# Top-k searches by bisection: the sample's with one bit a round on ScalarE alone, the prompt's as separate chains on VectorE and on ScalarE with GpSimd

## The chip, the cores and the metric

One core of one Trainium2 chip runs the kernel. The metric is device microseconds of one launch, from start to end; the median of three runs is given. One execution more was run with the hardware profiler; its durations, waits and starts are what the prediction works with. A core has five engines that each work through a list of instructions in order: TensorE (PE, matrix products), VectorE (DVE), ScalarE (ACT, functions of one input), GpSimd (POOL) and SyncE (SP, transfers). GpSimd also issues the indirect gathers. An instruction waits at the head of its engine's list until what it needs is there, and all that stands behind it waits with it.

## The reference

One inference step of a layer with two groups of heads on the same normalised input of 1024 prompt tokens and 32 sample tokens (8 sequences of 4). Group A is attention over the 256 keys with the highest index score; group B is retention, chunk by chunk. Cut to what matters here:

```python
def _index_select(qi, wi, ki, qpos, kpos, topk):
    s = jnp.einsum('bqhd,bsd->bqhs', qi, ki) * (D_IDX ** -0.5)
    score = jnp.einsum('bqh,bqhs->bqs', wi, jax.nn.relu(s))
    valid = kpos[None, None, :] <= qpos[None, :, None]
    score = jnp.where(valid, score, -jnp.inf)
    top_val, top_idx = lax.top_k(score, topk)
    return top_idx, jnp.isfinite(top_val)
```

For the prompt, a query block of 128 tokens has 128 to 1024 keys; for the sample, each of 32 queries has 8192 cached keys, read by page, and its new ones. The chosen keys go into a softmax attention; of retention only the chunked products matter here: each of four head pairs projects queries and keys, then values and gates, for 8 token blocks and the sample.

## The kernel before, in words

The whole is one function, `tile_step`. A scheduler that simulates the kernel while it is built lists the instructions of each engine; what is written under `tc.high_priority()` is preferred. The stages by time: normalisation, transposes, the index projections and the prompt's index scores (`index_scores`, to about 176 us); the **key stage** (176 to 348), which gathers the sample's cached index keys; **retention** (348 to 641), four head pairs; the sample's selection and both attentions (from 593 to 840, overlapping retention's end); the output projection and the gates at the end.

**The prompt's search.** `bisect_prompt` (L618) is a generator, `bp`, that finds for each of 128 rows in 6 query blocks (384, 512, 640, 768, 896 and 1024 keys wide, `NB`) the 256th largest score, bit by bit. The scores' upper halves are copied as bf16 to `x16` and searched in 15 rounds; the lower halves of the scores that equal the result so far, as `y16`, in 16 rounds. In a round, `count` (L631) counts for each block the scores that reach the block's test value: the two largest blocks (`NA`) on ScalarE, as a Sign whose sum is accumulated (L644), the other four on VectorE (L648). VectorE turns the sums of signs into counts (L652, with the constant `halfn`) and then moves the test values of all six blocks in one go (L667 and L669; L690 to L693). So both engines meet in each round. Behind the search stands a mask for each block.

**The key stage.** A loop over 8 batches and two halves (L768) gathers 128x2048 of keys on GpSimd into `kx` (L772, two buffers), transposes them on TensorE (L782), copies them on ScalarE to `kT` (L783), multiplies them by the index queries (`pox`, L786) and applies relu on ScalarE (L789). `head_sum` and `by_key` sum over heads and write the scores to memory. Between, `unit` runs the projections `pb` (L252 to L254) of attention, and each half steps `bp` by about 1.5 rounds.

**The sample's search.** `bisect_sample` (L807), the generator `bss`, loads the scores as 128 partitions of 2080 (each query's on four partitions and for 8 batches) and does the same search twice over 16 bits. A round finds two bits with three test values: two Signs on ScalarE over all 2080 (L844), with their bias made by an Identity each (L865) from values that GpSimd prepares (L870 and L877), and for the middle value three counts on VectorE over 704, 688 and 688 (`jv`, L883) with one small step each (L887). A matmul with a constant 128x128 matrix (`totals`, `stot`, L849) adds up the partitions of a query, a Sign on the totals (L893) tells which tests hold, and VectorE moves the middle (L894). Eight rounds make a search.

**Retention.** For each head pair (L1368) the projection passes `pqk` (L262 to L264, three products each, 8 token blocks) with rotary steps on VectorE (L973 to L975) and GpSimd (L977, L978), then `pvg` with gates on ScalarE (L988) and the chunk products (L994 to L1005, L1395 to L1406). After each token block, `steps(hp)` (L1354) steps a search: in head pair 0 one of `bss` and two of `bp`, later one of `ss`. What is left of `bp` and of `bss` is written out when head pair 1 begins.

**The selection.** `sample_select` (L1097), the generator `ss`, starts from the found threshold: comparisons of all scores (L1133, L1134), prefix sums by a scan (L1142) and matmuls (`pfx`, L1148), corrections (L1156 to L1165), products `pdf` (L1175), then a loop of 11 rounds that makes the list of chosen keys (`oh` L1185, `psl` L1187, `le` L1191, L1195 to L1199). The list drives the gathers of cached keys and values (L1086) for the sample's attention, which runs mixed with the prompt's (L1471 to L1531).

Of the kernel before, what the change touches and what calls it, by code (L numbers as in the profile page):

```python
# [10 lines left out]
F32 = mybir.dt.float32  # L11
# [9 lines left out]
T = 1024  # L21
# [21 lines left out]
def _const_table():  # L43
# [36 lines left out]
    put("halfn", np.tile((np.arange(3, 9) * 64.0)[None, :], (128, 1)))  # L80
# [40 lines left out]
def tile_step(ctx: ExitStack, tc: tile.TileContext, I, O):  # L121
# [496 lines left out]
    def bisect_prompt():  # L618
# [16 lines left out]
        V = nc.vector  # L635

        def count(src, thr, op, scale=None):


            for j, o, n in lens[::-1]:  # L640
                t = thr if isinstance(thr, float) else thr[:, j:j + 1]
                if scale and j >= NB - NA:
                    js = bs.tile([128, 2 * T], BF16, tag="rk", bufs=1, name="js")
                    nc.scalar.activation(js[:, :n], src[:, o:o + n], AF.Sign, bias=t, scale=-scale,  # L644
                                         accum_out=cnt[:, j:j + 1])
                    continue
# [3 lines left out]
            if scale:  # L650
                a = slice(NB - NA, NB)
                V.scalar_tensor_tensor(cnt[:, a], cnt[:, a], -0.5, C("halfn")[:, a], op0=ALU.mult, op1=ALU.add)  # L652

# [9 lines left out]
        V.tensor_scalar(cand, tb_, 1 << 30, None, op0=ALU.bitwise_xor)  # L663
        for bit in range(30, 15, -1):
            count(x16, cand.bitcast(F32), ALU.is_ge, 1.0 + 2.0 ** -10)

            V.tensor_scalar(gb, cnt, float(TOPK), float(1 << bit), op0=ALU.is_lt, op1=ALU.mult)  # L667
            if bit > 16:
                V.scalar_tensor_tensor(cand, gb, 1 << (bit - 1), cand, op0=ALU.bitwise_xor, op1=ALU.bitwise_xor)  # L669
            else:  # L670
                V.tensor_tensor(tb_, cand, gb, op=ALU.bitwise_xor)
            yield
# [14 lines left out]
        V.memset(cf, float(1 << 15))  # L687
        for bit in range(15, -1, -1):
            count(y16, cf, ALU.is_ge, 1.0 + 2.0 ** -18)
            V.tensor_tensor(ge, cnt, need, op=ALU.is_ge)  # L690
            V.scalar_tensor_tensor(v, ge, float(1 << bit), v, op0=ALU.mult, op1=ALU.add)
            if bit:
                V.tensor_scalar(cf, v, float(1 << (bit - 1)), None, op0=ALU.add)  # L693
            yield
# [112 lines left out]
    def bisect_sample():  # L807
# [15 lines left out]
        nc.sync.dma_start(jk.bitcast(F32)[:, :128], I["const"][:, CW + 384:CW + 512])  # L823
        groupr = ss_.tile([128, 128], F32R, name="groupr")
        nc.gpsimd.tensor_copy(groupr, jk.bitcast(F32)[:, :128])
        group = groupr.bitcast(F32)
        cand, gb = (bits[:, i:i + 1] for i in range(2))
        sm = ss_.tile([128, 11], F32, name="ssm")
        cnt, sg, ng, c65, tu, v, need, te, k1, k2, bias = (sm[:, i:i + 1] for i in range(11))
        sgn = ss_.tile([128, 4], F32R, name="sgn")  # L830
# [3 lines left out]
        def count(thr, op):  # L834
# [3 lines left out]
            nc.tensor.matmul(t, group, cnt, start=True, stop=True)  # L838
            return t

        def signs(src, bias, j):

            with nc.allow_low_precision(reason="whole numbers up to NX"):
                nc.scalar.activation(jk, src, AF.Sign, bias=bias, accum_out=sgn[:, j:j + 1])  # L844

        def totals():

            t = bank("stot", "t")[:, 0:4]
            nc.tensor.matmul(t, groupr, sgn, start=True, stop=True)  # L849
            return t  # L850

        def search(src, k, mid):


            s = float(1 << 14)
            b = None
            V.memset(mid, 2 * s - 0.5)
            pre = ss_.tile([128, 4], F32, tag="pre", bufs=2, name="pre")
            for j in range(2):
                nc.gpsimd.memset(pre[:, j:j + 1], 0.5 - (3 - 2 * j) * s)  # L860
            for r in range(8):
                if r:
                    b = pre[:, 2:4]
                    for j in range(2):
                        nc.scalar.activation(b[:, j:j + 1], up, AF.Identity, bias=pre[:, j:j + 1], scale=-2.0 * s)  # L865
                        signs(src, b[:, j:j + 1], j)
                    if r < 7:
                        pre = ss_.tile([128, 4], F32, tag="pre", bufs=2, name="pre")
                        for j in range(2):
                            nc.gpsimd.tensor_scalar(pre[:, j:j + 1], b[:, j:j + 1], 0.75 * s * (1 - 2 * j), None,  # L870
                                                    op0=ALU.add)
                else:
                    for j in range(2):
                        signs(src, pre[:, j:j + 1], j)
                    p0, pre = pre, ss_.tile([128, 4], F32, tag="pre", bufs=2, name="pre")
                    for j in range(2):
                        nc.gpsimd.tensor_scalar(pre[:, j:j + 1], p0[:, j:j + 1], 0.75 * s * (1 - 2 * j), None,  # L877
                                                op0=ALU.add)
                c2 = ss_.tile([128, 5], F32, tag="c2", bufs=2, name="c2")
                part = -float(NX)  # L880
                for j, c, w in ((0, 0, 704), (1, 704, 688), (2, 1392, 688)):
                    jv = ss_.tile([128, 704], BF16, tag="jv", bufs=1, name="jv")
                    V.tensor_scalar(jv[:, :w], src[:, c:c + w], mid, None, op0=ALU.is_ge, op1=ALU.add,  # L883
                                    accum_out=c2[:, j:j + 1])
                    to = c2[:, 3 + j:4 + j] if j < 2 else sgn[:, 2:3]
                    with nc.allow_low_precision(reason="whole numbers up to NX"):
                        V.tensor_scalar(to, c2[:, j:j + 1], 2.0, part, op0=ALU.mult, op1=ALU.add)  # L887
                    part = to
                t = totals()

                st = ss_.tile([128, 4], F32, tag="st4", bufs=2, name="st4")
                up = st[:, 3:4]
                nc.scalar.activation(st[:, 0:3], t[:, 0:3], AF.Sign, bias=k, accum_out=up)  # L893
                V.scalar_tensor_tensor(mid, up, s / 2, mid, op0=ALU.mult, op1=ALU.add)  # L894
                s /= 4
                yield
# [8 lines left out]
        yield from search(u16, k1, tu)  # L905
        V.tensor_scalar(bias, tu, -1.0, -0.5, op0=ALU.mult, op1=ALU.add)
        signs(u16, bias, 0)
        t = totals()[:, 0:1]
# [10 lines left out]
        yield from search(u16, k2, v)  # L919
# [10 lines left out]
        nc.tensor.matmul(tot, group, cnt, start=True, stop=True)  # L930
# [8 lines left out]
        sel, eq, rk = (jk.bitcast(F32)[:NS, i * NS:i * NS + NS] for i in range(3))  # L939
# [414 lines left out]
    def steps(hp):  # L1354

        with tc.high_priority():
            step(bss if hp == 0 else ss)
# [385 lines left out]
```

## Time and profile before

| | before |
|---|---|
| three runs | 1080.88, 1080.19, 1079.3 us (median 1080.19) |
| profiled execution: its time, and its span | 1084.95 us, 1083.1 us |
| granted TensorE clock, mean | 0.964 |
| TensorE busy | 1005.3 us (93%) |
| weight loads | 845.4 us (78%) |
| VectorE busy | 765.1 us (71%) |
| ScalarE busy | 572.4 us (53%) |
| GpSimd busy | 292.4 us (27%) |
| instructions | 20067 |

A row that names a group (`L844 ACT ACTIVATE sjk<-su,pre`) has the line, the engine, the operation, and the tile written from the tiles read. In rows of one tile, `203/208/1322` are the shortest, the median and the longest in ns, then the first and the last start. In a row of waits, the engine and line that waited stands before `<-`, what ended the wait behind it. In tables by stretch, the columns follow the engines in the order of the table above, each with busy us and the number of instructions; then the granted clock, the share of the DMA engines and GB/s. The share of an engine over the whole span is a mean over stages that have different limits.

### The profile page before, as it was taken

How to read it: one execution, taken by the hardware profiler on the slowest of the kernel's cores; microseconds unless marked ns; L12 is line 12 of the kernel's file. 1: busy time of each engine (PE TensorE's matmuls, PEld its weight loads, DVE VectorE, ACT ScalarE, POOL GpSimd, SP SyncE). 2: the span in 40 equal slices, each digit the busy share in tenths (PEclk: the TensorE clock that was granted, in tenths of full speed). 3: DMA queues.
4: the chain of work that ended last, by engine and by line, in shares of the span. 5: the costliest groups of instructions: out<-in, count | busy, mean ns of one | idle time of the engine just before them, and what ended most of it. 6: DMA issues, size and time to landing. Idle time of an engine off the chain costs nothing.

```text
span 1083.1 us, 20067 instructions
## 1 busy us (share of the span) xinstructions
PE 1005.3 (93%) x7377; PEld 845.4 (78%) x7377; DVE 765.1 (71%) x2262; ACT 572.4 (53%) x1216; POOL 292.4 (27%) x301
## 2 busy tenths in 40 slices
PE   3899997988998889999999986899999799999998
PEld 2899997766776788888888954566665799999998
DVE  6847778989889998968769879677663622683332
ACT  5545564976798356877832335555554432442210
POOL 3102223111201532424425215544331421122110
PEclk9999999989999999999999975899999899999999
DMA  8211235536343311300321544434211511332211
GB/s 285 65 59 50 78 107 176 180 116 203 125 161 103 74 40 40 80 18 26 79 81 25 141 119 110 133 87 115 58 50 61 144 60 40 115 125 81 84 41 41
DMA packets 98308, 102.24 MB, mean 94 GB/s; under 512 B 21346, under 2 KB 88386, under 8 KB 95906
## 3 DMA queue, kind: packets, MB, share of 16 engines
q1 hardware_dynamic: 92450, 74.74, 23.2%
q0 software_dynamic: 5760, 26.22, 7.8%
q8 instruction: 58, 0.95, 0.4%
q14 instruction: 40, 0.33, 0.1%
HBM read 79.25 MB, written 21.68 MB: 93 GB/s over the span
## 4 chain that ended last, share of the span: by engine, by line
PE 67%; DVE 14%; issue 6%; ACT 6%; DMA 4%; POOL 2%; SPq 0%; POOLq 0%; DVEq 0%; ACTq 0%
PE pb L252 4%; PE pb L253 4%; PE pb L254 4%; PE pg L262 3%; PE pg L264 3%; PE pg L263 3%; PE ob L1519 3%; PE ptp L1511 2%; PE pvg L262 2%; PE po L262 2%; PE po L263 2%; PE pvg L264 2%; PE po L264 2%; PE pox L786 2%; PE pvg L263 2%
## 5 line engine op out<-in xcount | busy, mean ns | idle before, releaser
L1086 POOL DMA_INDIRECT kvs<-in_cache_kv,idx x64 | 63.2, 987 | 87.1 <-ACT pT L1516 39.2
L262 PE MATMUL pqk<-whi_qkb,xh 128*128 128x256 f32 x256 | 74.3, 290 | 3.5 <-DVE rp L975 3.2
L262 PE MATMUL po<-whi_o,yTh 128*128 128x256 f32 x256 | 74.0, 290 | 3.9 <-DVE x L1606 3.4
L262 PE MATMUL pvg<-whi_vgb,xh 128*128 128x256 f32 x256 | 75.2, 294 | 1.1 <-ACT sg L988 1.1
L264 PE MATMUL pvg<-whi_vgb,xl 128*128 128x256 f32 x256 | 74.7, 292 | 0.0
L264 PE MATMUL pqk<-whi_qkb,xl 128*128 128x256 f32 x256 | 73.9, 289 | 0.0
L263 PE MATMUL pvg<-wlo_vgb,xh 128*128 128x256 f32 x256 | 73.7, 288 | 0.0
L264 PE MATMUL po<-whi_o,yTl 128*128 128x256 f32 x256 | 73.7, 289 | 0.0
L263 PE MATMUL pqk<-wlo_qkb,xh 128*128 128x256 f32 x256 | 73.5, 287 | 0.0
L263 PE MATMUL po<-wlo_o,yTh 128*128 128x256 f32 x256 | 73.3, 287 | 0.0
L262 PE MATMUL pg<-whi_g,yTh 128*128 128x256 f32 x256 | 72.7, 284 | 0.0
L264 PE MATMUL pg<-whi_g,yTl 128*128 128x256 f32 x256 | 72.3, 282 | 0.0
L263 PE MATMUL pg<-wlo_g,yTh 128*128 128x256 f32 x256 | 72.2, 282 | 0.0
L844 ACT ACTIVATE sjk<-su,pre 128x2080 bf16<-128x2080 uint16 x32 | 64.8, 2025 | 5.0 <-DVE su L903 4.7
L1504 ACT ACTIVATE L<-L,mn 128x128 f32<-128x128 f32 (+7 forms) x64 | 49.5, 775 | 20.9 <-DVE mn L1501 17.7
L1700 DVE TENSOR_TENSOR sgm<-pu,sgm 128x256 f32<-128x256 f32 x32 | 13.6, 424 | 64.5 <-PE pu L264 55.3
L497 DVE SCALAR_TENSOR_TENSOR score<-r,wi,score 128x384 f32<-128x384 f32 (+5 forms) x42 | 44.2, 1052 | 20.7 <-ACT r L493 19.6
L262 PEld LDWEIGHTS pqk<-whi_qkb,xh 128*128 128x128 f32 x256 | 49.0, 191 | 7.4 <-issue 4.9
L262 PEld LDWEIGHTS po<-whi_o,yTh 128*128 128x128 f32 x256 | 49.9, 195 | 5.6 <-DVE x L1606 3.6
L1516 ACT COPY pT<-ptp 128x512 f32<-128x512 f32 x54 | 31.3, 581 | 41.9 <-PE ptp L1511 33.4
L648 DVE TENSOR_SCALAR_CACHE_REDUCE jk<-mask,cf 128x768 bf16<-128x768 uint16 (+1 forms) x64 | 51.9, 812 | 2.0
L1699 ACT ACTIVATE sgm<-pg 128x256 f32<-128x256 f32 x32 | 12.3, 383 | 75.9 <-PE pg L264 67.8
(525 smaller groups left out, 3471.3 us busy)
## 6 DMA issues: line engine op xcount, KB each, us to landing
wraw_qkb<-in_w_in SPq DMA_DIRECT2D x16, 256.0 KB
wraw_vgb<-in_w_in SPq DMA_DIRECT2D x16, 256.0 KB
wraw_o<-in_w_out SPq DMA_DIRECT2D x8, 512.0 KB
qas<-qas_d SPq DMA_DIRECT2D x8, 512.0 KB
xr<-in_x_prompt SPq DMA_DIRECT2D x8, 512.0 KB
wraw_g<-in_w_ple_gate SPq DMA_DIRECT2D x8, 512.0 KB
out_y_prompt<-sgm SPq DMA_DIRECT2D x32, 128.0 KB
qas_d<-qst SPq DMA_DIRECT2D x8, 384.0 KB
```

Of the source, the lines that this page charges most:

```text
L252: nc.tensor.matmul(pt[:m, :n], wh, xh[:, k, ts], start=(k == 0), stop=False)
L253: nc.tensor.matmul(pt[:m, :n], wh, xl[:, k, ts], start=False, stop=False)
L254: nc.tensor.matmul(pt[:m, :n], wl, xh[:, k, ts], start=False, stop=(k == KC - 1))
L262: nc.tensor.matmul(pt[:, :n], ah, hi[:, k, :n], start=(k == 0), stop=False)
L263: nc.tensor.matmul(pt[:, :n], ah, lo[:, k, :n], start=False, stop=False)
L264: nc.tensor.matmul(pt[:, :n], al, hi[:, k, :n], start=False, stop=(k == kc - 1))
L497: nc.vector.scalar_tensor_tensor(sc, r[:, :n], wi[:, qb, h:h + 1], sc, op0=ALU.mult, op1=ALU.add)
L648: V.tensor_scalar(jk[:, :n], src[:, o:o + n], t, None, op0=op, op1=ALU.add, accum_out=cnt[:, j:j + 1])
L844: nc.scalar.activation(jk, src, AF.Sign, bias=bias, accum_out=sgn[:, j:j + 1])
L1086: return nc.gpsimd.indirect_dma_start(out=dst, out_offset=None, in_=kvflat, in_offset=bass.IndirectOffsetOnAxis(ap=idx, axis=0))
L1504: behind[0] = nc.scalar.activation(L[:, :n], L[:, :n], AF.Exp, bias=least, scale=-1.0, accum_out=sm[:, i4:i4 + 1])
L1519: nc.tensor.matmul(ob[64 * o:64 * o + 64, :256], vtok[:, kb, kv * 64:kv * 64 + 64], pT[:, o * 256:o * 256 + 256], start=(kb == 0), stop=(k ...
```

## The change

**The prompt.** `count` serves the four small blocks on VectorE alone, and VectorE moves only their test values. Each of the two large blocks has a chain of its own: ScalarE's Sign accumulates into a column of a new tile `lt`, and GpSimd makes the next test value in three small steps (128x1): it adds the next bit, makes from the sum of signs what has to be taken back, and takes it back. The test value lies in two columns by turns (`tst`, in the second search `low2`). The bits' values are in `dl`, made from the constant `pow2`, which takes `halfn`'s place.

**The sample.** A search has 16 rounds of one bit. A round is one Sign over 2080 on ScalarE, the matmul `stot`, a Sign on its column and an Identity that makes the next bias, both on ScalarE too. The counts and the middle on VectorE and the steps on GpSimd go. The step of `bss` in `steps` is two rounds in head pair 0.

**Small things.** `group` has a tile and a load of its own with two matrices, `sel`, `eq` and `rk` of the new keys have tiles of their own, `sgn` has two columns.

```diff
 def bisect_prompt():
+        def signs(src, j, thr, scale):
+            j, o, n = lens[j]
+            js = bs.tile([128, 2 * T], BF16, tag="rk", bufs=1, name="js")
+            less = lt[:, j - NB + NA:j - NB + NA + 1]
+            nc.scalar.activation(js[:, :n], src[:, o:o + n], AF.Sign, bias=thr, scale=-scale, accum_out=less)
+            return less, n
-        def count(src, thr, op, scale=None):
+        def count(src, thr, op, blocks=lens):
...
         for bit in range(30, 15, -1):
-            count(x16, cand.bitcast(F32), ALU.is_ge, 1.0 + 2.0 ** -10)
-            V.tensor_scalar(gb, cnt, float(TOPK), float(1 << bit), op0=ALU.is_lt, op1=ALU.mult)
+            count(x16, ct, ALU.is_ge, small)
+            V.tensor_scalar(gb[:, A], cnt[:, A], float(TOPK), float(1 << bit), op0=ALU.is_lt, op1=ALU.mult)
...
+            for j in large:
+                a = j - NB + NA
+                t0, t1 = test[a]
+                less, n = signs(x16, j, t0.bitcast(F32), 1.0 + 2.0 ** -10)
+                back = kept_[:, a:a + 1]
+                if bit > 16:
+                    G.tensor_scalar(half(t1), half(t0), dl[:, a, bit - 17:bit - 16], None, op0=ALU.add)
+                G.tensor_scalar(back, less, float(n - 2 * TOPK), dl[:, a, bit - 16:bit - 15],
+                                op0=ALU.is_gt, op1=ALU.mult)
+                if bit > 16:
+                    G.tensor_scalar(half(t1), half(t1), back, None, op0=ALU.subtract)
+                    test[a] = [t1, t0]
...
         for bit in range(15, -1, -1):
-            count(y16, cf, ALU.is_ge, 1.0 + 2.0 ** -18)
-            V.tensor_tensor(ge, cnt, need, op=ALU.is_ge)
+            count(y16, cf, ALU.is_ge, small)
+            V.tensor_tensor(ge[:, A], cnt[:, A], need[:, A], op=ALU.is_ge)
...
+            for j in large:
+                less, n = signs(y16, j, t0, 1.0 + 2.0 ** -18)
+                G.tensor_scalar(nxt, t0, float(1 << (bit - 1)) - float(1 << bit) if bit else -1.0, None,
+                                op0=ALU.add)
+                G.tensor_scalar(keep, less, k2[:, a:a + 1], float(1 << bit), op0=ALU.is_le, op1=ALU.mult)
+                G.tensor_tensor(nxt, nxt, keep, op=ALU.add)
...
 def bisect_sample():
-        def search(src, k, mid):
-            for r in range(8):
...
+        def search(src, k):
+            V.memset(bias, 0.5 - (1 << 15))
+            for bit in range(15, -1, -1):
+                t = signs(src)
+                nc.scalar.activation(st, t, AF.Sign, bias=k)
+                if bit:
+                    nc.scalar.activation(bias, st, AF.Identity, bias=bias, scale=-float(1 << bit) / 2)
                 yield
...
     def steps(hp):
         with tc.high_priority():
-            step(bss if hp == 0 else ss)
+            step(bss if hp == 0 else ss, 2 if hp == 0 else 1)
```

What the change does to the lists of the engines is shown at three places. The first is GpSimd's list in the key stage. Before, the gathers of index keys (`kx`) stood there with the low halves of weights (`wlo_ga`) and nothing else:

```order
L772 DMA kx<-in_cache_kidx,kidx 128x2048 x2
L177 TENSOR_TENSOR wlo_ga_1861<-wraw_ga_1862,whi_ga_1860 128x1024
L177 TENSOR_TENSOR wlo_ga_1861<-wraw_ga_1866,whi_ga_1860 128x1024
L772 DMA kx<-in_cache_kidx,kidx 128x2048 x6
L177 TENSOR_TENSOR wlo_ga_2353<-wraw_ga_2354,whi_ga_2352 128x1024
```

After, in the same list, the steps of the two chains (`tst` the test value, `lt` the sum of signs and what is taken back) stand between the gathers:

```order
L693 TENSOR_SCALAR tst<-tst,dl 128x1
L819 DMA kx<-in_cache_kidx,kidx 128x2048
L694 TENSOR_SCALAR lt<-lt,dl 128x1
L697 TENSOR_SCALAR tst<-tst,lt 128x1
L693 TENSOR_SCALAR tst<-tst,dl 128x1
L694 TENSOR_SCALAR lt<-lt,dl 128x1
L697 TENSOR_SCALAR tst<-tst,lt 128x1
L819 DMA kx<-in_cache_kidx,kidx 128x2048
```

Thirteen of the 16 gathers now have steps ahead of them and behind them.

The second place is VectorE's list where the selection compares all scores (`eq` and `sel` from `X`). Before, this was in head pair 3's first pass, right behind rotary steps (`rp` from `pqk`):

```order
L1005 TENSOR_TENSOR sm<-second,cst 128x128
L973 TENSOR_TENSOR rp_1_7013<-pqk,cst 128x256
L974 TENSOR_TENSOR rp_1_7014<-pqk,cst 128x4x32
L975 TENSOR_TENSOR rp_1_7014<-pqk,cst 128x4x32
L1133 TENSOR_TENSOR eq<-X_4981,tq 128x32x64
L1134 TENSOR_TENSOR sel<-X_4981,tq 128x32x64
```

After, it is in the same head pair's second pass, among the chunks' decay products (`sm` from `ret` and `second`):

```order
L1017 TENSOR_TENSOR sm<-second,cst 128x128
L276 TENSOR_TENSOR sh_vg_7218<-pvg,sh_vg_7218 32x256
L1145 TENSOR_TENSOR eq<-X_4962,tq 128x32x64
L1146 TENSOR_TENSOR sel<-X_4962,tq 128x32x64
L1127 COPY wbias<-wb_4964 128x128
L1128 COPY wbias<-wb_4964 128x32
L1414 COPY sbd_3393<-ret 64x64 x2
L1017 TENSOR_TENSOR sm<-ret,cst 128x128
```

The comparisons moved behind all rotary steps of the last head pair, into the pass whose chunk products wait for `sm`.

The third place is TensorE's list around the selection's first prefix product (`pfx`). Before, it stood in the projections `pqk` of head pair 3:

```order
L1068 MATMUL dst<-vm,qk_8_6381 64x512
L262 MATMUL pqk<-whi_qkb_6402,xh 128x256
L263 MATMUL pqk<-wlo_qkb_6403,xh 128x256
L264 MATMUL pqk<-whi_qkb_6402,xl 128x256
L1148 MATMUL pfx<-sm_5028,cst 128x32
L262 MATMUL pqk<-whi_qkb_6402,xh 128x256
```

After, it stands in the second pass, among the projections `pvg` and the chunk products (`ret`):

```order
L264 MATMUL pvg<-whi_vgb_6924,xl 128x256
L262 MATMUL pvg<-whi_vgb_6924,xh 128x256
L1416 MATMUL ret<-sbd_3393,qkT 128x128
L1160 MATMUL pfx<-sm_5009,cst 128x32
L1418 MATMUL ret<-vv_1_7294,sm 128x64 x2
L263 MATMUL pvg<-wlo_vgb_6925,xh 128x256
```

The selection's prefix and difference products now all stand behind head pair 3's first pass; of the 1536 projection matmuls of retention, the first `pfx` stands behind 1314 before and behind 1465 now. The last total of the search (`stot`) stands behind 1112 of them before and behind 1223 now.

More of the change, by code (lines that the diff above doesn't have):

```diff
@@ L634, in bisect_prompt @@
         ge = bs.tile([128, NB], F32, name="ge")
-        V = nc.vector
-        def count(src, thr, op, scale=None):
-            for j, o, n in lens[::-1]:
-                t = thr if isinstance(thr, float) else thr[:, j:j + 1]
[L642 to L646, printed above, removed]
+        lt = bs.tile([128, 5 * NA], F32, name="lt")
+        k2, kept_, low2 = lt[:, NA:2 * NA], lt[:, 2 * NA:3 * NA], lt[:, 3 * NA:5 * NA]
+        V, G = nc.vector, nc.gpsimd
+        A = slice(0, NB - NA)
+        small, large = lens[:NB - NA], range(NB - NA, NB)
+        def signs(src, j, thr, scale):
[5 more added lines that the diff above has]
+        def count(src, thr, op, blocks=lens):
+            for j, o, n in blocks[::-1]:
+                t = thr if isinstance(thr, float) else thr[:, j:j + 1]
                 jk = bs.tile([128, T], BF16, tag="jk", bufs=1, name="jk")
@@ L822, in bisect_sample @@
         bits = ss_.tile([128, 2], I32, name="sbits")
[L823 removed]
+        group = ss_.tile([128, 2, 128], F32, name="group")
+        nc.sync.dma_start(group, I["const"][:, CW + 384:CW + 640])
         groupr = ss_.tile([128, 128], F32R, name="groupr")
[L825 to L826 removed]
+        nc.gpsimd.tensor_copy(groupr, group[:, 0])
         cand, gb = (bits[:, i:i + 1] for i in range(2))
[L828 to L830 removed]
+        sm = ss_.tile([128, 12], F32, name="ssm")
+        cnt, sg, ng, c65, tu, v, need, te, k1, k2, st, bias = (sm[:, i:i + 1] for i in range(12))
+        sgn = ss_.tile([128, 2], F32R, name="sgn")
         ct = cand.bitcast(F32)
@@ L837, in count, with signs @@
             t = bank("stot", "t")[:, 0:1]
-            nc.tensor.matmul(t, group, cnt, start=True, stop=True)
+            nc.tensor.matmul(t, group[:, 0], cnt, start=True, stop=True)
             return t
-        def signs(src, bias, j):
+        def signs(src):
             with nc.allow_low_precision(reason="whole numbers up to NX"):
-                nc.scalar.activation(jk, src, AF.Sign, bias=bias, accum_out=sgn[:, j:j + 1])
-        def totals():
-            t = bank("stot", "t")[:, 0:4]
+                nc.scalar.activation(jk, src, AF.Sign, bias=bias, accum_out=sgn[:, 0:1])
+            t = bank("stot", "t")[:, 0:2]
@@ L849, in totals @@
             nc.tensor.matmul(t, groupr, sgn, start=True, stop=True)
-            return t
-        def search(src, k, mid):
[L855 to L860, printed above, removed]
-            for r in range(8):
[L862 to L895, printed above, removed]
@@ L896, in search @@
+            return t[:, 0:1]
+        def search(src, k):
[5 more added lines that the diff above has]
+                    nc.scalar.activation(bias, st, AF.Identity, bias=bias, scale=-float(1 << bit) / 2)
                 yield
@@ L904, in bisect_sample @@
         yield
-        yield from search(u16, k1, tu)
+        yield from search(u16, k1)
+        V.scalar_tensor_tensor(tu, st, 0.5, bias, op0=ALU.mult, op1=ALU.subtract)
         V.tensor_scalar(bias, tu, -1.0, -0.5, op0=ALU.mult, op1=ALU.add)
-        signs(u16, bias, 0)
-        t = totals()[:, 0:1]
+        t = signs(u16)
         V.tensor_scalar(k2, t, float(8 * NX - 2 * TOPK + 1), None, op0=ALU.add)
@@ L918, in bisect_sample @@
         yield
-        yield from search(u16, k2, v)
+        yield from search(u16, k2)
+        V.scalar_tensor_tensor(v, st, 0.5, bias, op0=ALU.mult, op1=ALU.subtract)
         V.scalar_tensor_tensor(v, v, sg, c65, op0=ALU.mult, op1=ALU.add)
@@ L929, in bisect_sample @@
         tot = bank("stot", "t")[:, 0:1]
-        nc.tensor.matmul(tot, group, cnt, start=True, stop=True)
+        nc.tensor.matmul(tot, group[:, 0], cnt, start=True, stop=True)
         V.tensor_copy(te, tot)
@@ L938, in bisect_sample @@
         xn = Xt[:NS, 2048:]
-        sel, eq, rk = (jk.bitcast(F32)[:NS, i * NS:i * NS + NS] for i in range(3))
+        sel = ss_.tile([NS, NS], F32, name="nsel")
+        eq = ss_.tile([NS, NS], F32, name="neq")
+        rk = ss_.tile([NS, NS], F32, name="nrk")
         V.tensor_scalar(sel, xn, tf, None, op0=ALU.is_gt)
```

37 lines of the change are left out of this document (29 added, 8 removed).

## Prediction

> **What bounds the kernel now.** I read the table of stretches first, cut where the stages change (key stage of both searches 180 to 348, retention head pairs 0 to 3 from 348 to 641, attention after that). Columns: stretch, length, then busy time and instructions of TensorE, its weight loads, VectorE, ScalarE and GpSimd, granted clock, DMA share, GB/s.
>
> ```profile
> 180.00:348.00 168.00, 153.40 (x927) 109.09 (x926) 146.99 (x429) 131.26 (x219) 27.11 (x27) 0.95 0.48 159
> 348.00:420.00 72.00, 63.83 (x490) 58.51 (x490) 70.98 (x184) 33.94 (x71) 24.71 (x29) 0.95 0.21 52
> 420.00:557.00 137.00, 135.51 (x1129) 121.36 (x1130) 108.39 (x401) 103.96 (x235) 48.23 (x84) 1.00 0.20 52
> 593.00:641.00 48.00, 45.05 (x355) 39.66 (x351) 36.73 (x119) 18.78 (x61) 14.41 (x14) 0.96 0.59 156
> 641.00:680.00 39.00, 26.25 (x143) 17.49 (x142) 35.81 (x165) 21.09 (x58) 16.05 (x16) 0.57 0.35 92
> ```
>
> TensorE is the engine that fills most stretches; but in head pair 0 (348 to 420) VectorE is busy 70.98 of 72 us while TensorE is at 63.83, and in 641 to 680 VectorE is busy 35.81 of 39 while TensorE has 26.25 and its clock falls to 0.57. These two stretches are VectorE's. In the middle, 420 to 557, TensorE is at 135.51 of 137: what leaves VectorE there can hardly pay. The second view was TensorE's waits, in 348 to 420 (first two rows) and after 641 (last row): us in total, times, longest.
>
> ```profile
> PE pqk L262 <- DVE rp L975: 3.2, 3, 1.4
> PE stot L849 <- DVE sgn L887: 3.2, 1, 3.2
> PE psl L1187 <- DVE lo__5807 L1195: 3.1, 1, 3.1
> ```
>
> All three name VectorE. The third view was the start of each projection pass, which gives the length of a head pair from one engine's clock:
>
> ```profile
> 347.83 0.39 PE L262 MATMUL pqk<-whi_qkb,xh 128*128 128x256 f32 x1
> 380.63 0.36 PE L262 MATMUL pvg<-whi_vgb,xh 128*128 128x256 f32 x1
> 420.59 0.39 PE L262 MATMUL pqk<-whi_qkb,xh 128*128 128x256 f32 x1
> 452.99 0.39 PE L262 MATMUL pvg<-whi_vgb,xh 128*128 128x256 f32 x1
> 487.43 0.36 PE L262 MATMUL pqk<-whi_qkb,xh 128*128 128x256 f32 x1
> ```
>
> Head pair 0 takes 72.8 us (32.8 + 40.0), head pair 1 takes 66.8 (32.4 + 34.4). The same work, so 5.6 us of pair 0's second pass is VectorE's fullness there.
>
> **Key stage, the prompt's search.** Before, VectorE and ScalarE meet in each round. The waits in 176 to 348:
>
> ```profile
> DVE cnt L652 <- ACT js L644: 11.5, 14, 2.3
> ACT js L644 <- DVE cand L669: 7.2, 5, 3.1
> ACT js L644 <- DVE cf L693: 3.0, 4, 0.9
> ACT js L644 <- DVE mask L683: 2.7, 1, 2.7
> PE pox L786 <- ACT kT L783: 5.4, 2, 4.6
> ```
>
> The change takes away the first (11.5) and ScalarE's 12.9 us. But TensorE's stage is 153.40 of 168 with only 5.4 us of wait for ScalarE's key copies in this list, so little of it can reach the end. What comes in: the two large blocks are still counted by ScalarE's Signs, as many as before, and then go through three GpSimd steps a bit each. No such chain is in this trace; the nearest single-column GpSimd step is the sample search's. With it, the gathers that share GpSimd's list, and the Signs of the second search (shortest/median/longest in ns, then first and last start):
>
> ```profile
> L870 POOL TENSOR_SCALAR pre<-pre x24: 203/208/1322, 378.2 to 529.3; 128x1 f32<-128x1 f32 x24
> L772 POOL DMA_INDIRECT kx<-in_cache_kidx,kidx x16: 936/938/1474, 174.7 to 328.6; - x16
> L644 ACT ACTIVATE js<-mask,cf x32: 1028/1106/1192, 279.2 to 350.6; 128x1024 bf16<-128x1024 uint16 x16, 128x896 bf16<-128x896 uint16 x16
> ```
>
> A round of one chain is a Sign of 1.1 us and two GpSimd steps on the path (0.4; the third runs beside the Sign), and the two chains alternate, so ScalarE has the other block's Sign while GpSimd works: 2.2 us for both blocks, GpSimd's 1.2 us covered. If that cover is lost, because a gather of 0.94 us is ahead of a step, ScalarE stands, and behind its Sign stand the key copies (kT) that TensorE's key products wait for. Bounds: a gain of 8 (the 5.4 that TensorE waits for key copies, and most of the 3.2 that head pair 0 waits for its ropes, if VectorE is done with the prompt earlier) to a loss of 8 (13 gathers are listed between the steps, 12.2 us at 0.94; a third of it I take as covered by the other block's Sign). I take 0, the middle: the rows price both ends alike.
>
> **Head pair 0.** The sample search's counts on VectorE (jv, three a round) go. First the table of stretches for those counts alone (after the length, VectorE's busy time), then the Signs of that search:
>
> ```profile
> 348.00:420.00 72.00, 11.20 (x24) 0.95 0.21 52
> 420.00:557.00 137.00, 33.51 (x72) 1.00 0.20 52
> L844 ACT ACTIVATE sjk<-su,pre x32: 2012/2028/2057, 368.6 to 541.5; 128x2080 bf16<-128x2080 uint16 x32
> ```
>
> 11.2 us of 70.98 leave this stretch, but the order puts other VectorE work of the prompt's mask ahead of the first rope, so I don't count the whole. What can be had is 5.6 (pair 0 against pair 1). I take −4, bounds −6 and 0. ScalarE's Signs stay 32 of 2.03 us, no change. In 420 to 557, where 33.5 us of counts leave, TensorE has 1.5 us left: I take 0, bound −1.5. GpSimd's preparing steps (L870) leave an engine that is busy 48 of 137 us there, and the new tiles and the one load of the constant matrix come once, ahead of the search: 0 for these.
>
> **More totals on TensorE.** 16 rounds of one bit instead of 8 of two, for two searches: 32 small matmuls in place of 16, each with the following Sign on ScalarE. What one takes of TensorE's stream:
>
> ```profile
> 376.97 0.28 PE L264 MATMUL pqk<-whi_qkb,xl 128*128 128x256 f32 x1
> 377.08 0.17 PE L849 MATMUL stot<-sgn,groupr 128*128 128x4 f32 x1
> 377.11 0.37 PE L262 MATMUL pqk<-whi_qkb,xh 128*128 128x256 f32 x1
> ```
>
> By the starts it is 0.03 us, by its duration 0.17, and the matmul behind it is 0.08 longer than its like. 16 more at 0.1 to 0.25: 1.6 to 4.0; I take 2.5. The Sign on a total now waits for TensorE 32 times, not 16; behind it on ScalarE stand the gates that TensorE's second passes wait for, and that wait is small today:
>
> ```profile
> PE pvg L262 <- ACT sg L988: 1.1, 1, 1.1
> ```
>
> Doubled it is 1.1 more, which the upper bound of 4.0 holds.
>
> **The search ends later.** A round of the sample's search was two Signs of 2.03 us, a total, a Sign on it and an Identity in a row; two rounds of one bit have the same two long Signs and the rest of the chain twice. Two rounds are stepped where one was, but the order shows the last total some 110 of the 1536 projection matmuls later (behind 1223, before 1112), and the selection's first prefix product, which was in head pair 3's first pass (behind 1314), in its second (behind 1465). So the selection's long VectorE steps, which started at 569.9 us, start in head pair 3's second pass:
>
> ```profile
> L1133 DVE TENSOR_TENSOR eq<-X,tq x1: 2573/2573/2573, 569.9 to 569.9; 128x2048 bf16<-128x2048 f32 x1
> L1134 DVE TENSOR_TENSOR sel<-X,tq x1: 2545/2545/2545, 572.4 to 572.4; 128x2048 bf16<-128x2048 f32 x1
> L1142 DVE TENSOR_TENSOR_SCAN cx<-eq x1: 4637/4637/4637, 577.2 to 577.2; 128x2112 f32<-128x2112 bf16 x1
> L1156 DVE TENSOR_TENSOR cx<-cx,sm x1: 2279/2279/2279, 592.2 to 592.2; 128x2048 f32<-128x2048 f32 x1
> L1191 DVE TENSOR_TENSOR le<-psl,cst x11: 405/539/558, 634.3 to 665.7; 128x384 bf16<-128x384 f32 x10, 128x256 bf16<-128x256 f32 x1
> ```
>
> The four steps are 12.0 us and stood before 593. With them the stretch 593 to 641 has 36.73 + 12.0 = 48.8 us of VectorE work in 48: full, and TensorE waits for VectorE's decay products there. The list loop (le, eleven rounds) ran from 634.3 to 665.7, 3.1 us a round; two or three rounds that lay before 641 now lie behind it, 6 to 9 us in a stretch that is VectorE's already. The 33.5 us that VectorE has free in 420 to 557 let none of this run earlier, since the selection waits for the search. I take +6.5, the low end of these rounds; bounds 0 (the prompt's attention fills the time instead) and +15 (nine of the loop and six of the full pass).
>
> [...] VectorE and GpSimd met once beside head pair 0:
>
> ```profile
> 364.26 4.28 DVE L903 SCALAR_TENSOR_TENSOR su<-sjk,Xt 128x2080 uint16<-128x2080 uint16 x1
> 366.31 2.54 POOL L977 TENSOR_TENSOR qk<-rp,rp 128x128 f32<-128x128 f32 x1
> 368.81 0.45 POOL L978 TENSOR_TENSOR qk<-rp,rp 128x128 f32<-128x128 f32 x1
> ```
>
> The same GpSimd operation took 2.54 us beside VectorE's two-input step and 0.45 after it. [...]
>
> **Sum.** 0 − 4 + 0 + 2.5 + 6.5 = +5.0. The profiled execution took 1084.95 us; its like after the change is 1089.95. The three runs shown have a median of 1080.19, 4.8 below it, so the same step gives 1085.2.
>
> **Rivals.** 0.2% of this time, 2.2 us, is about what a measurement of this kernel can tell from no change.
>
> 1. *VectorE's relief pays* (faster). The counts were in the one pass where VectorE was full, and TensorE's waits name VectorE. Key stage −4, head pair 0 −6, middle −1.5, totals +1.6, and the selection is absorbed by the prompt's attention (0): −9.9, 1070.3. For it: 70.98 of 72. Against it: 35.81 of 39 in the stretch that the selection moves to. It decides if the first list round starts before 641.
> 2. *Nothing reaches the end* (same). TensorE's 135.51 of 137 hides the search, and pair 0 gives 2.5 that the totals take: 1080.2.
> 3. *GpSimd's list couples the chains to the gathers* (slower). A gather waits there for its buffer, and all steps behind it wait too. 13 gathers at 0.94 give 12 more than the forecast: 1097. It decides if ScalarE's wait for GpSimd in the key stage is more than the 12.9 us that it had for VectorE.
> [...]
>
> **How the numbers follow.** The forecast gets 0.40, as the order shows the selection later and the trace shows VectorE full where it goes; rival 1 0.28; rival 2 0.14; rival 3 0.12; rival 4 0.06. Faster is rival 1: 0.28. Same is rival 2: 0.14. Slower is the rest: 0.58. The forecast's own terms reach from −13.9 to +27; the range takes rival 1 as its low end, 1070, and rival 3 and a little as its high end, 1098, which leaves out the outer part of both tails, about 2 in 10.
>
> **What would show it.** Right: the selection's first comparison starts past 593 (569.9 before), the first list round past 641 (634.3 before), VectorE above 45 us in 593 to 641; head pair 0 under 70 us (72.8 before); 33 totals with no more than 4 us between them and their neighbours. Wrong: the key stage's length differs by more than 8 us; the stretch from 348 on moves as one block with the list rounds at their old distance; ScalarE's largest wait in the key stage names a GpSimd step (rival 3), or GpSimd's steps average above 0.3 us (rival 4).

## The result, and the profile after

The changed kernel took 1091.76 us (median of four runs, 1086.59 to 1096.07) against 1079.74 for the kernel before: a ratio of 1.0109, 95% interval 1.0068 to 1.0149, so 12 us slower, 7 to 16. Six more runs later gave 1094.52 against 1079.53, 1.0129 (1.0100 to 1.0157). The first four runs of the changed kernel lie further apart than those of before (9.5 us against 2.8), the later ones do not (5.5 against 7.3). One run of experiment 2's kernel took 5199.27 us and is in no ratio.

The table of stretches of the changed kernel (first trace, profiled execution 1086.59 us, the fastest of its runs; columns as before):

```profile
180.00:348.00 168.00, 148.51 (x872) 107.34 (x870) 145.06 (x414) 128.38 (x215) 75.77 (x200) 0.94 0.46 154
348.00:420.00 72.00, 62.96 (x481) 54.84 (x479) 56.31 (x125) 34.55 (x70) 24.93 (x29) 0.95 0.24 61
420.00:557.00 137.00, 136.27 (x1121) 122.01 (x1122) 65.33 (x275) 101.02 (x221) 43.60 (x62) 1.00 0.19 48
593.00:641.00 48.00, 43.30 (x338) 38.76 (x339) 42.38 (x110) 17.52 (x56) 12.95 (x23) 0.97 0.53 142
641.00:680.00 39.00, 25.15 (x171) 18.07 (x172) 37.98 (x177) 19.01 (x51) 6.13 (x6) 0.59 0.34 93
```

VectorE falls from 70.98 to 56.31 in 348 to 420 and from 108.39 to 65.33 behind it, as the change says. But fixed windows no longer hold the same work: in the first one TensorE issues 872 matmuls, 927 before. The kernel is behind already when retention begins. So I cut both kernels at the same work, the first projections of head pairs 0 and 1 and of head pair 3's second pass. Each kernel has two traces, since one execution is not enough here: before's first (1084.95) was 5 us over its runs, the changed kernel's first 5 under. The second ones (1080.16 and 1095.45) are close to the medians. Lengths in us, from the starts of these matmuls:

| | before 1084.95 | before 1080.16 | changed 1086.59 | changed 1095.45 |
|---|---|---|---|---|
| start to head pair 0 | 347.8 | 345.7 | 356.7 | 361.4 |
| head pair 0 | 72.8 | 72.7 | 71.7 | 69.9 |
| head pair 1 to head pair 3's second pass | 172.4 | 172.4 | 172.7 | 173.3 |
| from there to the end | 490.1 | 487.7 | 483.7 | 489.1 |

With the two traces near the medians: +15.7 − 2.8 + 0.9 + 1.4 = +15.3, the whole difference of the two spans (1093.7 and 1078.4). The loss is ahead of head pair 0, in the key stage; it is there in the other pair of traces too (+8.9).

### The profile page after: what moved, and what is told of

Same layout as the page of the kernel before. It is cut to its first block, busy times and chain, and to the rows that moved or that the text cites. A ratio compares the mean times of both kernels' runs of the same rounds, so it can differ in the third digit from the quotient of the medians.

```text
span 1084.8 us, 20107 instructions
## 1 busy us (share of the span) xinstructions
PE 1000.8 (92%) x7393; PEld 848.9 (78%) x7393; DVE 717.2 (66%) x2080; ACT 580.1 (53%) x1218; POOL 328.4 (30%) x455
## 4 chain that ended last, share of the span: by engine, by line
PE 64%; DVE 23%; DMA 5%; issue 3%; ACT 3%; POOL 1%; SPq 1%; ACTq 0%; DVEq 0%; POOLq 0%
DVE jk L653 9%; PE ob L1531 4%; PE ptp L1523 3%; PE pb L252 3%; PE pb L253 3%; PE pb L254 3%; PE pg L262 3%; PE pg L264 3%; PE pg L263 3%; PE po L262 2%; PE po L264 2%; PE po L263 2%; PE pvg L262 2%; PE pvg L263 2%; PE pvg L264 2%
## 5 line engine op out<-in xcount | busy, mean ns | idle before, releaser
L1098 POOL DMA_INDIRECT kvs<-in_cache_kv,idx x64 | 67.5, 1055 | 78.2 <-ACT pT L1528 28.4
L262 PE MATMUL pg<-whi_g,yTh 128*128 128x256 f32 x256 | 72.8, 284 | 0.9 <-ACT sgm L1711 0.9
L891 ACT ACTIVATE sjk<-su,ssm 128x2080 bf16<-128x2080 uint16 x33 | 67.0, 2030 | 2.2 <-DVE su L912 0.8
L493 ACT ACTIVATE r<-si 128x384 f32<-128x384 f32 (+5 forms) x48 | 36.3, 758 | 30.2 <-PE si L351 29.0
```

What stands on the lines that cost most here:

```text
L262: nc.tensor.matmul(pt[:, :n], ah, hi[:, k, :n], start=(k == 0), stop=False)
L493: nc.scalar.activation(r[:, :n], s[:, :n], AF.Relu)
L1098: return nc.gpsimd.indirect_dma_start(out=dst, out_offset=None, in_=kvflat, in_offset=bass.IndirectOffsetOnAxis(ap=idx, axis=0))
```

## Where the key stage loses

The same cut as a table of stretches, from 176 us to the start of head pair 0, in the second trace of before:

```profile
176.00:345.67 169.67, 153.85 (x945) 110.63 (x944) 149.99 (x433) 133.00 (x222) 30.54 (x29) 0.98 0.49 162
```

and in the second trace of the changed kernel:

```profile
176.00:361.36 185.36, 161.15 (x947) 113.88 (x945) 161.76 (x441) 135.84 (x226) 81.17 (x211) 0.94 0.44 147
```

TensorE has the same work, 945 and 947 matmuls. It stands 24.2 us in place of 15.8 (length less busy time), 8.4 more; and it is busy 161.15 in place of 153.85, 7.3 more, for the same matmuls. The granted clock says why: 161.15 x 0.94 is 151.5, 153.85 x 0.98 is 150.8. In this pair of traces half of the loss is waiting, half is a slower clock. In the first pair it is 5.9 us of waiting (20.5 against 14.6) and 3.0 of busy time (160.22 against 157.23), so the share of the clock changes from one execution to the next. TensorE's waits in this stretch, before (second trace):

```profile
PE pox L786 <- ACT kT L783: 5.7, 2, 4.8
PE kvt L405 <- ACT kvs L401: 2.9, 1, 2.9
PE pox L786 <- DVE vnew L411: 1.6, 1, 1.6
PE kvt L405 <- DVE xe L761: 0.7, 1, 0.7
```

and changed (second trace):

```profile
PE kvt L405 <- ACT kvs L401: 6.0, 2, 3.4
PE pox L833 <- ACT kT L830: 5.4, 1, 5.4
PE pox L833 <- DVE xe L808: 4.7, 2, 3.4
PE pox L833 <- DVE kvs L407: 2.1, 1, 2.1
```

The wait for ScalarE's key copies is what it was. New are waits for short VectorE copies (xe, kvs), and ScalarE's kvs, which had itself waited 4.9 us for a VectorE step (kst):

```profile
ACT kvs L401 <- DVE kst L420: 4.9, 1, 4.9
```

What delays such a copy is seen in the timeline of the changed kernel (start, duration). TensorE transposes the scores (pxt), VectorE has to copy them (xe), and the next key product (pox) stands behind the copy, since pxt and pox share the kernel's two banks of tag `t`; it waited 3.42 us for it (last row):

```profile
322.16 0.60 PE L804 MATMUL pxt<-cst,ys 128*128 128x128 f32 x4
326.33 1.01 DVE L653 TENSOR_SCALAR_CACHE_REDUCE jk<-mask,cf 128x768 bf16<-128x768 uint16 x1
330.37 1.01 DVE L653 TENSOR_SCALAR_CACHE_REDUCE jk<-mask,cf 128x768 bf16<-128x768 uint16 x1
331.31 0.61 DVE L808 COPY xe<-pxt 128x64 f32<-128x64 f32 x4
332.07 1.97 PE L833 MATMUL pox<-kT,qbd 128*64 128x512 f32 x4 [3.42 <-DVE xe L808]
```

The copy could start at 322.8; it starts at 331.31, because the counts of two rounds of the prompt's search and the first of a third stand ahead of it. In before's second trace the same copy came half a us behind its transposes:

```profile
310.80 0.60 PE L757 MATMUL pxt<-cst,ys 128*128 128x128 f32 x4
311.85 0.61 DVE L761 COPY xe<-pxt 128x64 f32<-128x64 f32 x4
```

So VectorE is not short of time, it is early with the wrong work: freed from ScalarE, it runs through its own rounds and meets TensorE's copies late. In VectorE's list, the counts that stand ahead of the eight xe copies are 40, 60, 72, 86, 103, 121, 128, 132 before, and 51, 66, 73, 101, 121, 136, 136, 136 now.

The clock is the other part. Three stretches of the changed kernel's second trace, around a wait of 3.4 us for kvs (222.1 to 225.5):

```profile
218.70:225.40 6.70, 3.40 (x26) 3.13 (x24) 6.46 (x19) 5.18 (x11) 4.43 (x13) 0.97 0.69 226
225.40:232.20 6.80, 6.24 (x20) 2.58 (x21) 6.49 (x19) 6.44 (x13) 3.53 (x11) 0.52 0.53 177
232.20:250.00 17.80, 17.56 (x112) 14.41 (x110) 17.09 (x44) 15.24 (x27) 9.41 (x23) 1.00 0.26 85
```

TensorE is busy 3.40 of 6.70 us, and for the next 6.8 us its clock is 0.52, though it is busy 6.24 us of them; then 1.00 again. This wait cost its own length and, by my estimate (half of 6.8), some 3 us more. Not every wait does: one of 2.6 us for kvs, which ended at 215.6, brought no lower clock (1.00 from 211 to 218.7). And the kernel before has the same wait in both its traces, with two outcomes. The wait, then the stretch behind it, first and second trace:

```profile
221.21 0.90 PE L405 MATMUL kvt<-cst,kvs 128*128 128x128 f32 x3 [2.99 <-ACT kvs L401]
220.50:227.30 6.80, 6.09 (x19) 2.84 (x20) 4.13 (x15) 5.15 (x10) 0.00 (x0) 0.50 0.45 166
```

```profile
220.27 0.55 PE L405 MATMUL kvt<-cst,kvs 128*128 128x128 f32 x3 [2.92 <-ACT kvs L401]
220.50:227.30 6.80, 5.91 (x38) 2.40 (x36) 5.58 (x20) 6.80 (x12) 0.00 (x0) 1.00 0.42 159
```

Half the clock and 19 matmuls after a wait of 2.99 us, the full clock and 38 after one of 2.92. So nearly the same wait at one place cost the clock in one execution and not in the other; what decides this is not shown.

## Experiments

**1. The whole change again** (a second trace; no edit).

> The changed kernel as it is, to see the spread of its executions: four of them took 1086.6 to 1096.1 us, four of before 1078.1 to 1080.9. Theory A (the key stage is longer by 9 us, because VectorE's own search runs ahead and the short VectorE steps that TensorE waits for come late in it): a ratio near 1.011, and in the trace the first projection of head pair 0 again near 356.7 us against 347.8. Theory B (what the prediction had: the selection's late start is what costs, 6.5 us): the loss lies behind 641 us, with the output projection starting 5 us or more later than 838.7. In the first trace of this kernel it started at 838.3; if this trace has it past 843, that one was an exception.

Measured: 1094.52 us, ratio 1.0129 (1.0100 to 1.0157). Head pair 0 starts at 361.4, the output projection at 843.9, against 345.7 and 830.9 in before's second trace. 843.9 is past the 843 that theory B had named, but the 15.7 us of the key stage have become 13.0 there: between the two points nothing was lost, and 2.3 us were behind the output projection's start (249.8 against 247.5). The key stage ended later than theory A had it, too (361.4, not near 356.7). The first trace was simply the faster one, by 4.7 us in the key stage and 5.4 from head pair 3's second pass on.

**2. and 3. The two parts of the change, each alone.** The first has the diff's part on `bisect_prompt` and its constant, the second has the rest.

> The prompt's part alone, the sample's search as before. Theory A: slower by 5 to 10 us in the key stage, head pair 0's first projection near 356 us. Theory B: the search ends no later than before (in the order its last total stands behind 1062 projection products, 1112 before), so no loss behind 641 us, and the whole within 3 us of before.

> The sample's part alone, the prompt's search as before. Theory A: the key stage as before (head pair 0 starts within 2 us of 347.8), and the whole within 3 us of before or faster by the 2 to 6 us of head pair 0. Theory B: the last total stands behind 1217 projection products, so the selection is as late as in the whole change (607.6 us), and the whole is slower by 5 to 9 us.

Measured: the prompt's part alone 1105.76 us, 1.0228 (1.0197 to 1.0260); the sample's part alone 1086.70, 1.0062 (1.0040 to 1.0085). Head pair 0 starts at 358.3 with the prompt's part and at 345.2 with the sample's: the key stage's loss belongs to the prompt's part alone. By the ratios the two losses, 24.6 and 6.7 us, don't add up to the whole one, 13.9, and neither theory had the 24.6. By its trace the prompt's part alone loses 12.6 us in the key stage, 3.2 in head pair 0 and 9.3 from there to head pair 3's second pass. With the prompt's part alone the selection's comparisons start at 581.0, inside head pair 3's first pass, which takes 41.8 us (36.1 before); in the whole change they start at 610.8, and this pass takes 33.6. By its size the sample's result fits theory B. By its trace only 2.1 us are lost from head pair 3's second pass on (489.8), and 4.9 in head pair 0 (77.6 against 72.7), where I had put a gain: TensorE's waits there are for ropes and decay products that stand behind the prompt's masks in VectorE's list,

```profile
PE pqk L262 <- DVE rp L940: 6.0, 1, 6.0
PE ret L1360 <- DVE sm L970: 3.7, 1, 3.7
```

Why the two parts together have a shorter head pair 0 (69.9) than each alone (75.9 and 77.6) is not shown.

**4. The chains' small steps on VectorE.**

```diff
-        V, G = nc.vector, nc.gpsimd
+        V, G = nc.vector, nc.vector
```

> The whole change, with the three small steps of each large block's chain on VectorE instead of GpSimd. Theory A: the chains are still apart from the small blocks, but VectorE gets 184 steps of some 0.13 us (24 us) back; the key stage is as long as in the whole change or longer, 0 to +15 us. Rival C (GpSimd's list, with its gathers, holds up the chains): the key stage becomes shorter than in the whole change by 5 us or more.

Measured: 1096.71 us, 1.0142 (1.0113 to 1.0172); head pair 0 starts at 364.4. No gain, so rival C falls: GpSimd and its gathers don't hold the chains up. The run alone would not settle it, since the Signs now waited 13.8 us for the chains' steps in VectorE's list. But the changed kernel's trace says the same: of ScalarE's idle time ahead of the Signs (js), GpSimd ended this much:

```profile
  POOL tst L697: 0.4, 1
```

**5. The kernel before again** (for a second trace).

> The kernel before once more, for a second trace of it: its profiled execution took 1084.95 us, 5.4 above the median of its runs, so stages compared with it alone can be off by as much. If the 5.4 lie in one stage, that stage's comparison changes: theory A needs the key stage to end (first projection of head pair 0) within 3 us of 347.8 again; if it ends near 343, the whole change loses 18 there and not 13.5.

Measured: 1080.16 us, head pair 0 at 345.7. Of the 4.8 us by which before's first trace was longer, 2.2 lie in the key stage and 2.4 from head pair 3's second pass on (to the output projection 5.5 longer, behind it 3.0 shorter).

**6. A wait put back.** VectorE copies both sums of signs in each round before it moves its own test values (the second search alike):

```diff
...
             count(x16, ct, ALU.is_ge, small)
+            both = [signs(x16, j, test[j - NB + NA][0].bitcast(F32), 1.0 + 2.0 ** -10) for j in large]
+            V.tensor_copy(cnt[:, NB - NA:], lt[:, :NA])
-            V.tensor_scalar(gb[:, A], cnt[:, A], float(TOPK), float(1 << bit), op0=ALU.is_lt, op1=ALU.mult)
+            V.tensor_scalar(gb, cnt, float(TOPK), float(1 << bit), op0=ALU.is_lt, op1=ALU.mult)
...
-                less, n = signs(x16, j, t0.bitcast(F32), 1.0 + 2.0 ** -10)
+                less, n = both[a]
...
```

> The whole change, with one wait put back: in every round of the prompt's search VectorE copies the two sums of signs before it moves the small blocks' test values, so it cannot run ahead of ScalarE's chains. It is 31 copies of some 0.13 us more work. In the order, the counts that stand ahead of the eight copies of scores (xe) go from 51, 66, 73, 101, 121, 136, 136, 136 to 42, 62, 72, 92, 108, 129, 136, 136 (before: 40, 60, 72, 86, 103, 121, 128, 132). Theory A (VectorE's free run is the loss): the key stage ends at 350 to 354 in place of 361.4, and the whole is 5 to 10 us faster than the whole change, a ratio of 1.003 to 1.008. Rival C (the chains with GpSimd themselves are slow): as slow as the whole change or slower, ratio 1.013 or more, since a wait is added and none goes.

Measured: 1100.74 us, 1.0188 (1.0158 to 1.0219), a miss for theory A as a whole, and by its ratio what rival C had. But rival C's chains are in this run too, and the key stage did become shorter, 355.6 against 361.4, by a wait more and 31 copies more; TensorE stands 19.5 us in it, not 24.2. But head pair 0 takes 78.7 (69.9 in the whole change), and from head pair 3's second pass to the end it is 498.3 (489.1).

**7. The selection made late, in the kernel before.**

```diff
-        tqb = tq[:, :, None].to_broadcast([128, NS, 64])
+        tq2 = p2.tile([128, NS], F32, name="tq2")
+        V.scalar_tensor_tensor(tq2, late[1][:, :NS], 0.0, tq, op0=ALU.mult, op1=ALU.add)
+        tqb = tq2[:, :, None].to_broadcast([128, NS, 64])
...
```

`late[1]` is the first block of values of head pair 3's second pass, and the selection is stepped from that block on.

> The kernel before with its own searches, in which the selection is made late: its first comparison also reads a value of head pair 3's second pass (times zero), so it can start only past 598 us (569.9 before, 610.8 in the whole change). Nothing else is changed. Theory B (the late selection costs what the prediction had, 6.5, bounds 0 to 15): a ratio of 1.004 to 1.010. Theory A: the attention stage takes the delay up, as in the whole change's trace, where retention ended 14.5 us late and the output projection began 5.2 late: ratio 0.998 to 1.002.

Measured: 1086.32 us, 1.0065 (1.0041 to 1.0089). The comparisons start at 595.2, 28 us later than in before's second trace, and nothing else is moved on purpose: +7.0 us by the ratio (4.4 to 9.6), as theory B had it. Its trace, the run of 1084.7 us, is 4.5 us longer than before's second one; 3.7 of them lie from head pair 3's second pass on (491.4 against 487.7). This pass, to the last chunk product, takes 53.6 us (48.1 before).

**8. and 9. The copies on ScalarE,** in the whole change and, as a control, in the kernel before.

```diff
-            nc.vector.tensor_copy(xe[:, t].rearrange("p i r u -> p r i u"), pv[:, :, :, t * 4:t * 4 + 4])
+            nc.scalar.copy(xe[:, t].rearrange("p i r u -> p r i u"), pv[:, :, :, t * 4:t * 4 + 4])
...
-        nc.vector.tensor_copy(st[:, 1, :nb], tp[:, :nb])
+        nc.scalar.copy(st[:, 1, :nb], tp[:, :nb])
...
```

> The whole change, with the copies in the key stage that TensorE waited for on VectorE (the scores xe, the transposed keys and values, the new ones) on ScalarE instead: 38 copies, some 10 us of ScalarE work, no arithmetic changed. Theory A (the copies came late because they stand behind VectorE's counts in its list): TensorE's waits for VectorE in the key stage (4.7 for xe, 2.1 for kvs and 0.5 in the last trace) go, and with them half-clock time; the key stage ends at 352 to 357 in place of 361.4, the whole is 4 to 9 us faster than the whole change. Rival D (ScalarE is the engine that is late, with its Signs ahead of its key copies): the key stage ends at 361 or later, since ScalarE gets more to do.

> The kernel before with the same copies on ScalarE, as the control for the run above: before, VectorE stood still for ScalarE in each round and its copies came in time. Theory A: key stage within 3 us of 345.7 and the whole within 0.3% of before. Rival D: the key stage longer by 4 us or more. If it is faster than before by over 0.3%, this is the version to keep.

Measured: 1101.62 us, 1.0187 (1.0154 to 1.0220), and 1105.06 us, 1.0221 (1.0191 to 1.0251). In the key stage the two move opposite ways: the changed kernel's ends at 351.8 in place of 361.4, before's at 357.8 in place of 345.7. The changed kernel with the copies on ScalarE, by the table of stretches and TensorE's longest waits there:

```profile
176.00:351.77 175.77, 157.01 (x957) 113.51 (x956) 149.12 (x398) 141.14 (x266) 81.80 (x212) 0.97 0.47 157
```

```profile
PE pox L833 <- ACT kT L830: 6.4, 2, 5.4
PE kvt L405 <- ACT kvs L401: 5.7, 2, 4.1
PE pxt L804 <- ACT rl L836: 2.0, 2, 1.5
```

The waits for VectorE are gone, the clock is back from 0.94 to 0.97, and ScalarE, with 5 us more to do, does not make the stage longer. The key stage lost 9.6 of its 15.7 us, and rival D falls for the changed kernel. The move also changed VectorE's list: the counts ahead of the eight copies are now 53, 66, 72, 91, 108, 128, 136, 136. But experiment 6 has nearly these counts, with the copies on VectorE, and ends the key stage 3.8 us later (355.6). Before, where the copies were not late, ScalarE is the worse place for them (+12.1): theory A had 3 at most, and this run came out as rival D had it.

The whole did not become 4 to 9 us faster, as theory A had it, but has the ratio 1.0187 in place of 1.0129. What the key stage gained was given back: head pair 0 takes 78.2 us, so that head pair 1 starts at 430.0 (431.3 without the move, 418.4 before), and from head pair 3's second pass to the end it is 500.0. In head pair 0 a mask step of VectorE ran beside GpSimd's split of weights (`wlo_qkb`) and took 5.13 us for a block of 128x896 (0.42 in the whole change); TensorE then waited 5.7 us for a decay product that stood behind the masks. In the whole change it is the next block's step, 128x1024, that runs beside the split: 5.26 us, 0.43 in experiment 8. No wait of TensorE follows it there. So the late copies account for most of the key stage's loss, and not for the time of the whole. The step and the split in experiment 8:

```profile
391.55 5.13 DVE L758 TENSOR_SCALAR mask<-gt 128x896 bf16<-128x896 bf16 x1
391.70 4.72 POOL L177 TENSOR_TENSOR wlo_qkb<-wraw_qkb,whi_qkb 128x1024 fp32r<-128x1024 f32 x2
```

In 6 and 8 alike the list loop runs later than in the whole change. Its rows in the whole change (second trace), in experiment 7, in 6 and in 8, one fence each:

```profile
L1203 DVE TENSOR_TENSOR le<-psl,cst x11: 407/536/557, 657.7 to 688.0; 128x384 bf16<-128x384 f32 x10, 128x256 bf16<-128x256 f32 x1
```

```profile
L1193 DVE TENSOR_TENSOR le<-psl,cst x11: 407/539/558, 647.7 to 680.7; 128x384 bf16<-128x384 f32 x10, 128x256 bf16<-128x256 f32 x1
```

```profile
L1206 DVE TENSOR_TENSOR le<-psl,cst x11: 407/539/549, 672.8 to 710.5; 128x384 bf16<-128x384 f32 x10, 128x256 bf16<-128x256 f32 x1
```

```profile
L1203 DVE TENSOR_TENSOR le<-psl,cst x11: 406/539/539, 671.8 to 709.9; 128x384 bf16<-128x384 f32 x10, 128x256 bf16<-128x256 f32 x1
```

Where the loop's last round starts by 698.4 (the other nine traces) the time from head pair 3's second pass to the end is 483.7 to 491.4; where it starts at 710 it is 498.3 and 500.0. Why the loop is so late in these two is not shown. No version here beats the kernel before.

## Why the prediction was right and wrong

It had the sign and a range that held the result, and a middle that was too low: +5.0 forecast, +12 measured. But its largest term is not what cost the time, and the stage that did was put at 0: that the sum came out slower, inside the range, is in good part luck.

- **Key stage: 0, bounds −8 and +8; measured +15.7 (+8.9 in the first traces).** This is the step that failed, by the prediction's own sign of a difference above 8 us. "I take 0, the middle: the rows price both ends alike" weighed ScalarE's waits against GpSimd's gathers. It didn't ask what VectorE does with the time in which it no longer waits: it goes on in its list, and in that list counts stood ahead of the copies that TensorE needs. Experiments 2 and 4 place the loss in the prompt's part and not in GpSimd, and 9.6 us of it went when the copies moved to ScalarE (experiment 8). The bound of +8 was priced by waits alone. The waits grew by 8.4 us (5.9 in the first traces); the lower clock, for which the sum has no term, added 7.3 (3.0).
- **Rival 3 had the place and not the cause.** ScalarE waited 0.4 us for GpSimd, where the rival asked for more than 12.9, and with the steps on VectorE the kernel was no faster.
- **Head pair 0: −4; measured −2.8** in the second traces (−1.0 in the first). VectorE's 71 us there became 51.5. The sign was right in the whole change, though only the second trace is under 70 us; with either part alone the pass became longer.
- **Middle 0 and totals +2.5; measured +0.9 together.** The 33 totals took 0.165 us each by their median, and from head pair 1 to head pair 3's second pass TensorE was busy 172.17 of 173.29 us:

```profile
L893 PE MATMUL stot<-sgn,groupr x33: 164/165/271, 385.9 to 583.1; 128*128 128x2 f32 x33
```

- **The late selection: +6.5; measured +1.4 in the whole change.** It came as forecast: the comparisons past 593, the first list round past 641.

```profile
L1145 DVE TENSOR_TENSOR eq<-X,tq x1: 2292/2292/2292, 607.6 to 607.6; 128x2048 bf16<-128x2048 f32 x1
L1203 DVE TENSOR_TENSOR le<-psl,cst x11: 407/539/557, 652.4 to 682.0; 128x384 bf16<-128x384 f32 x10, 128x256 bf16<-128x256 f32 x1
```

  VectorE in 593 to 641 was 42.38, under the 45 that I had named. Experiment 7 shows that the price was a real one for the kernel before (7.0). In the whole change, what the second pass of head pair 3 lost (51.3 against 48.1) the first one gained, since the selection had left it (33.6 against 36.1). Why the attention behind it took the rest up in one kernel and less of it in the other stays open.
- **Rival 4 (GpSimd's steps above 0.3 us on average).** The chains' GpSimd steps have a mean of 0.27 us (49.8 us for 184), below the 0.3 that I had set; the step of the sample's search from which I had priced the chains had a median of 0.208. The step with two tensors as inputs (L739) is no longer than the one with one input and constants (L736), and in experiment 4 it took 0.156 us on VectorE by its median, against 0.192 on GpSimd. Line, busy us and mean ns, in the changed kernel's second trace:

```profile
L736 POOL TENSOR_SCALAR lt<-lt 128x1 f32<-128x1 f32 x30 | 6.6, 221 | 2.3
L739 POOL TENSOR_TENSOR lt<-lt 128x1 f32<-128x1 f32 x30 | 5.7, 191 | 2.4
```

Some 6 us of the key stage's loss stayed with the copies on ScalarE (351.8 against 345.7). The traces show where. Cut at the first transposes of the scores (pxt; 223 to 234 matmuls after 176 us), the part ahead of the cut ends at 222.6 before, at 230.7 in the whole change, at 231.1 in experiment 8 and at 225.4 in experiment 6. The part behind it, to head pair 0, takes 123.1, 130.7, 120.7 and 130.2 us. So what experiment 8 saved lies behind the cut, and the 8 us ahead of it stayed. There ScalarE's kvs waited for VectorE's step kst (a difference, which stayed on VectorE) 4.9 us in the whole change and 6.1 in experiment 8; before, and in experiment 6 with its wait put back, it did not wait for kst at all. That makes kst the likely second late step. It was not moved alone, so this is not shown.

## What to carry to other kernels

When a change frees an engine from a wait, ask what it does next: an engine with a fixed list runs on into its own work, and the short steps that others wait for can come later although it has more time (here a copy that could start at 322.8 us started at 331.31). A wait that looks like waste may be what kept two lists in step, though putting one back did not win the time back here. And price a wait of TensorE with the clock that may follow it, not by its length alone (here 0.52 for 6.8 us after a wait of 3.4 us); compare more than one execution, since that part differs between them (0.50 and 1.00 after one wait of the kernel before).

## What was not expected of the hardware

After a wait of 2.99 us TensorE ran its next 6.8 us at half the clock (0.50) in one execution of the kernel before; after a wait of 2.92 us at the same place it kept the full clock (1.00) in another. In the changed kernel's key stage, with its longer waits, the same 947 matmuls were busy 160.22 and 161.15 us (mean granted clock 0.94 in both), against 157.23 and 153.85 for 949 and 945 before (0.95 and 0.98).

A mask step of VectorE over 128x896 bf16 took 5.13 us beside GpSimd's split of weights (experiment 8) and 0.42 without it (the whole change's second trace); the one over 128x1024 took 5.26 beside it (second trace) and 0.43 without it (experiment 8).
